# Hybrid retention/MoBA block: one Strassen unit of 512-column products for MoBA's values and the first retention gate, in place of two units of 256-column products

## The chip, the cores and the metric

The kernel runs on one core of one Trainium2 chip. The metric is the device time of one execution in microseconds (us), lower is better; it is given as the median of several executions. The engines are PE (TensorE: matmuls, and its weight loads as PEld), DVE (VectorE), ACT (ScalarE), POOL (GpSimd) and SP (SyncE, which here only issues transfers).

## The reference

One decoder layer in float32 on 512 tokens of width 1024:

```python
h = rmsnorm(x, norm1_w)
rq, rk, rv, rg, mq, mk, mv, ga, gb = split(h @ w_in)   # 512,512,1024,1024,512,512,512,1024,1024 columns
a = (silu(rg) * retention(rotary(rq), rotary(rk), rv)) @ w_ret_out     # 4 heads, 128 / 256 wide
b = moba_attention(rmsnorm(mq), rmsnorm(mk), mv) @ w_moba_out          # 8 heads of 64
x = x + (sigmoid(ga) * a + sigmoid(gb) * b) @ w_o
x = x + (silu(h2 @ w_ffn_gate) * (h2 @ w_ffn_up)) @ w_ffn_down         # h2 = rmsnorm(x, norm2_w)
```

With 512 tokens the MoBA selection takes every earlier block, so attention is plain causal attention. The change concerns the 512 columns `mv` and the first 512 of the 1024 columns `rg` (the gate of retention heads 0 and 1).

## The kernel before, in words

**Arithmetic.** Each float32 operand is split into a high and a low fp32r part, and each product is three matmuls (high x high, high x low, low x high: `mm3`). Most projections are done by Strassen's method (the class `Wino` keeps the sums of the activations): a unit makes four quarters of a result from seven quarter products instead of eight. The activations' pieces are kept for the whole first half. A weight piece is a tile of 128 x 1024 float32 (512 KB): it is loaded (`load_w`), where Strassen needs a sum of quarters a second transfer from POOL adds to it, or DVE adds two pieces (`make_sum`); then ACT writes the high part `wh` (line 418) and DVE the low part `wl`. Up to 3, sometimes 4, split pieces stand ahead of PE.

**Units.** `weight_plan` (line 87) lists the units in order. Kind "X" with 256-column halves gives 512 output columns: four quarters of 256 tokens x 256 columns. A product is one weight piece: 2 token tiles of 128 times 4 row tiles times 3 matmuls of 256 columns. Kind "X" with 512-column halves exists already for `w_o` and `w_ffn_down`: each quarter is 256 tokens x 512 columns, a product has two weight pieces and 2 x 2 x 2 x 3 matmuls of 512 columns, and each of its results takes two PSUM banks. `wino_prod` (line 780) issues a product and `wino_unit` (line 811) a unit. The order of the products is `NORMAL = "B11 T1 *1 T2 B21 B22 T3 / T4"`: the last one, T4, is put off and issued in the following unit, behind that unit's second product.

**Order of the work.** PE gets first the MoBA queries and keys (`tok_double`, 512-column matmuls), then the unit of `mv` (256-column, lines 1007 to 1020), then the units in the order of `ORDER` (line 44): rg0, rk0, rv0, gb0, rk1, rv1, rg1, gb1, b0, b1, ga0, a0, ga1, a1; then `w_o` and the feed-forward part. Here rk is a pair of rotary query and key units, ga and gb are the merge gates, a and b the two output projections.

**The background queue.** Everything else (norms, transposes, attention, retention) lies in one first-in, first-out list `bg`. `run_bg(1)` (line 708) takes one step of it after every 12 matmuls of 256 columns, or every 6 of 512 in a 512-column unit. This text calls such a place a slot. A 256-column unit has 14 slots, two to a product. The key's preparation takes 15 steps from the end of the key products on: 3 empty, `qk_scales`, four `k_norm`, 3 empty, four `k_transpose` (line 961). Attention's 38 steps (`att_step`) are appended by `mv_out` once the last quarter of `mv` is done, which is in unit rg0 behind T4. The steps of retention follow when `rv` is done (19 steps a pair of heads), and those of the gate (`gates`, line 1142) when `rg` and `rv` both are.

**Evacuation.** The class `Quarters` takes a 256-column unit's results out of PSUM: P1 is copied from bank X to bank Z (line 890), two negated intermediates go to SBUF (893, 896), DVE subtracts two, and the `out` function takes each finished quarter. `mv_out` scales by the row norm (line 1013), and `rg_unit` copies two of its quarters (line 1130).

**Space.** SBUF holds 47 tiles of 128 x 1024 float32, for weights and activations alike: a load waits until its slot is free. PSUM has 8 banks. One, `zbank`, is held from the start for bank Z. A side step (`side_ps`) takes a bank for itself. After the query unit `more_raws(EXTRA)` allows one more weight tile, 5 in all.

Of the kernel before, what the change touches and what calls it, by code (L numbers as in the profile page):

```python
# [38 lines left out]
PAHEAD = (6, 8)  # L39
STARTERS = 2  # L40
EXTRA = 1
OEXTRA = 5
FEXTRA = -2
ORDER = (("rg", 0), ("rk", 0), ("rv", 0), ("gb", 0), ("rk", 1), ("rv", 1), ("rg", 1), ("gb", 1), ("b", 0), ("b", 1), ("ga", 0), ("a", 0), ("ga", 1), ("a", 1))
RLAG = (1, 2, 3)
SLAG = (1, 1, 1)
ROT = 1
# [39 lines left out]
def weight_plan():  # L87

    units = []

    def feat(blocks):
        assert len(blocks) % 16 == 0  # L100
        for i in range(0, len(blocks), 16):
            units.append(("F", blocks[i:i + 16]))

    def group(name, col, kts):
        return [(name, k * P, col) for k in range(kts)]

    def wino(name1, col1, name2, col2, order=NORMAL):
        quarters = ((name1, col1, 0), (name2, col2, 0), (name2, col2, 4), (name1, col1, 4))
        units.append(("W", [(n, (k0 + k) * P, c + i * P) for n, c, k0 in quarters for i in (0, 1) for k in range(4)],
                      order))  # L110

    halves = (range(4), range(4, 8))

    def cols(col):
        units.append(("X", ("w_in", halves, col, 256), NORMAL))

    units += [("M", (C_MQ, 0)), ("M", (C_MQ, 4)), ("M", (C_MK, 0)), ("M", (C_MK, 4))]
    cols(C_MV)
    for name, i in ORDER:
        if name == "rg":  # L120
            cols(C_RG + 512 * i)
        elif name == "rv":
            cols(C_RV + 512 * i)
        elif name == "rk":
            wino("w_in", C_RQ + 256 * i, "w_in", C_RK + 256 * i)
        elif name == "a":
            feat(sum([group("w_ret_out", (4 * i + ct) * P, KT) for ct in range(4)], []))
        elif name == "b":
            feat(sum([group("w_moba_out", (4 * i + ct) * P, 4) for ct in range(4)], []))
        else:  # L130
            c = {"ga": C_GA, "gb": C_GB}[name] + 512 * i
            wino("w_in", c + 256, "w_in", c)
    units.append(("X", ("w_o", halves, 0, 512), ALONE))
    for c in range(len(CHUNKS)):
        fs = chunk_tiles(c)
        for f in fs[::2]:
            order = ENDING if f == fs[-2] else NORMAL
            if f < 4:
                order = (PLAIN, DOWN)[f // 2]
            wino("w_ffn_gate", f * P, "w_ffn_up", f * P, order)  # L140
        units.append(("X", ("w_ffn_down", (fs[::2], fs[1::2]), 0, 512), ALONE if c == len(CHUNKS) - 1 else DOWN))
    return units


# [25 lines left out]
def hybrid_block(ctx: ExitStack, tc: tile.TileContext, wall, xin, xtok, n2, cin, out):  # L170
# [15 lines left out]
    def big(name, dt=F32):  # L186
        return bp.tile([P, 1024], dt, name=name, tag="b")
# [14 lines left out]
    def main_ps():  # L202
        return pp.tile([P, 512], F32, name=nm("pm"), tag="bank")
# [7 lines left out]
    class Paced:  # L211


        def __init__(self, engine, cost):
            self.engine, self.cost = engine, cost
# [47 lines left out]
    def later(n, f):  # L263
        later_q.append([n, f])
# [454 lines left out]

    zbank = main_ps()  # L720

    def tok_double(mov, evac):

        pss = [main_ps() for _ in range(NT - 1)] + [main_ps() if cur[0] else zbank]
        lows = []
        for k in range(KT):
            for t in range(NT):
                m = ("A11", "A21", "A12", "A22")[k // 4 * 2 + t // 2]
                mm3(pss[t], tuple(x[:, t % 2 * P:t % 2 * P + P] for x in hW(m, k % 4)), mov(k), k == 0, k == KT - 1)
            advance(1)  # L730
            for l in lows:
                l()
            lows = [sums.pop(0)() for _ in range(SUMS) if sums and k < KT - 1 and cur[0]]
            run_bg(1)
        for t in range(NT):
            evac(t, pss[t])
        cur[0] += 2
# [73 lines left out]
    def wino_unit(w, ev, hooks={}):  # L811

        u = cur[0]
        cur[0] += 1
        order = plan[u][2].split()
        wide = plan[u][0] == "X" and plan[u][1][3] == 512
        banks = {}

        def bank(b):
            if b not in banks:  # L820
                z = zbank if b == "Z" else main_ps()
                banks[b] = [z, main_ps()] if wide else z
            return banks[b]

        def third(*x):
            ev.c22(*x)
            if "T4w" in order:
                ev.u3(*x)

        def first(*x):  # L830
            ev.p1(*([*x, bank("Z")] if seed else x))

        whole = "T4w" in order or "T4z" in order
        seed = not wide and order[1] != "B21"
        table = {"B11": ("X", "A11", True, False, first), "T1": ("Y", "S1", True, False, ev.p5),
                 "T2": ("X", "S2", False, False, ev.u2), "B21": ("Z", "A12", not seed, True, ev.c11),
                 "B22": ("Y", "S4", False, True, ev.c12), "T3": ("X", "S3", False, whole, third),
                 "T4": ("X", "A22", False, True, ev.c21),
                 "T4w": ("W", "A22", True, True, getattr(ev, "c21w", None)),
                 "T4z": ("Z", "A22", False, True, ev.c21)}  # L840

        def run(q):
            b, m, start, stop, out = table[q]
            wino_prod(w, u, bank(b), m, q.rstrip("wz"), start, stop, out,
                      bank("Z") if q == "T3" and "T4z" in order else None,
                      q == "T4z")

        rest = False
        for q in order:
            if q == "/":  # L850
                rest = True
            elif q[0] == "*":
                for _ in range(int(q[1:])):
                    wino_finish()
            elif rest:
                wpend.append(lambda q=q: run(q))
            else:
                run(q)
                if q in hooks:
                    hooks[q]()  # L860
# [22 lines left out]
    class Quarters:  # L883
# [27 lines left out]
        def c21(self, x):  # L911
            self.out(1, 0, x)


    mqT, mkT = {}, {}
    r1 = {}
# [59 lines left out]
        V.tensor_tensor(st["wqk"], vec[:, V_Q:V_Q + 1], vec[:, V_K:V_K + 1], ALU.mult)  # L976

    tok_double(lambda k: mw[k], qk_evac(0, qraw))
    more_raws(EXTRA)
    bg.append(norm1_rows)  # L980
    for g in range(4):
        bg.append(lambda g=g: q_transpose(g))
# [21 lines left out]
    for g in range(4):  # L1004
        bg.append(lambda g=g: k_transpose(g))

    mv = {}

    def mv_out(pair, u, x):
        for i in (0, 1):  # L1010
            t = 2 * pair + i
            mv[t, u] = (mv_ev.a, mv_ev.b)[u][:, t * 256:(t + 1) * 256]
            A.activation(mv[t, u], x[:, i * 256:(i + 1) * 256], AF.Copy, scale=st["r1"][:, t:t + 1])
        if (pair, u) == (1, 0):
            for n in range(len(items) + ATT[1]):
                bg.append(lambda n=n: att_step(n))

    wstate["cap"] = AHEAD
    mv_ev = Quarters(mv_out)
    wino_unit(hW, mv_ev)  # L1020


    srg_ev = {}
# [77 lines left out]
    def att_values(g):  # L1101

        ps = side_ps()
        for j in range(NT):
            for r in (0, 1):
                x, o = pt_tile(g, r, j)
                h = 2 * g + r
                T.matmul(ps[r * MDH:(r + 1) * MDH, j * P:], lhsT=mv[j, h // 4][:, h % 4 * MDH:(h % 4 + 1) * MDH],
                         rhs=x[:, o:o + S - j * P], start=j == 0, stop=j == NT - 1, skip_group_check=True)
        del pT[g]  # L1110
        moT[g] = split(f"moT{g}", ps, None, SLAG[0])
# [9 lines left out]
    moT = {}  # L1121


    srg = {}

    def rg_unit(n):
        def out(pair, i, x):
            if i == 0:
                y = ev.free if pair else ev.a[:, :512]
                A.copy(y, x)  # L1130
                x = y
            srg[2 * n + i, pair] = x
            if (pair, i) == (1, 0):
                gates(n)
                ret_done("rg")

        ev = Quarters(out)
        wino_unit(hW, ev)
# [164 lines left out]
    def ret_gate(h, pair):  # L1303
        x = srg[h, pair]
        for i in (0, 1):
            t = 2 * pair + i
            c = slice(i * 256, (i + 1) * 256)
            A.activation(x[:, c], x[:, c], AF.Silu, scale=st["r1"][:, t:t + 1])

    def ret_norm(h, pair):  # L1310
        o = ro[h, pair]
        for i in (0, 1):
            c = slice(i * 256, (i + 1) * 256)
            x = h * NT + 2 * pair + i
            A.activation(o[:, c], o[:, c], AF.Identity, scale=st["gn"][:, x:x + 1], bias=st["gb"][:, x:x + 1])
        later(1, lambda: V.tensor_tensor(o, o, srg[h, pair], ALU.mult))

    retT = {}

# [99 lines left out]
    def branch(cts, n, mov, evac):  # L1419
# [8 lines left out]
        "a": lambda n: branch(range(4 * n, 4 * n + 4), KT, retT, a_evac),  # L1428
        "b": lambda n: branch(range(4 * n, 4 * n + 4), 4, moT, b_evac),
    }  # L1430
    for name, n in ORDER:
        make[name](n)
    assert not bg
# [353 lines left out]
```

## Time and profile before

| | us |
|---|---|
| median of 3 runs | 779.98 (779.82 to 781.38) |
| the profiled execution, its own time | 780.48 |
| its span, first to last instruction | 778.4 |
| PE busy | 772.3 (99%) |
| DVE busy | 630.3 (81%) |
| ACT busy | 457.1 (59%) |
| POOL busy | 68.8 (9%) |

The profile is of one execution. Times count from the start of the span, which is some 2 us shorter than the execution. The granted TensorE clock is 0.999 on average. Line 222 is a helper through which all matmuls and most DVE instructions go, so they are told apart by their tiles: `pm` is a PSUM bank of the main products, `ps` one of a side step, `wh` and `wl` the parts of a weight piece, `raw` a weight piece as loaded.

### The profile page before, as it was taken

The numbers are of one execution on the slowest core, as the hardware profiler recorded it, in microseconds if no ns is written. First come the engines' busy times: TensorE is split into PE (matmuls) and PEld (weight loads), VectorE is DVE, ScalarE is ACT, GpSimd is POOL, SyncE is SP. The second block draws the span as 40 slices with busy tenths as digits, with TensorE's granted clock in tenths as the row PEclk, the third lists the DMA queues.
The fourth block names the chain that finished last, engine by engine and source line by source line (L and its number), as shares of the span: only waits on it lengthen the run. The fifth ranks groups of instructions, "written<-read, shape, count | busy, mean of one in ns | idle before, by whom it ended". The sixth has DMA issues, their size and how long they took to land.

```text
span 778.4 us, 13652 instructions
## 1 busy us (share of the span) xinstructions
PE 772.3 (99%) x5394; PEld 711.3 (91%) x5394; DVE 630.3 (81%) x959; ACT 457.1 (59%) x750; POOL 68.8 (9%) x83
## 2 busy tenths in 40 slices
PE   9999999999999999999999999999999999999997
PEld 6889988899999998989988899989999899988996
DVE  7988778897788687758589898899787987789787
ACT  8655677774695485635355675654554455654542
POOL 0000100010101000000001000111001110110000
PEclk9999999999999999999999999999999999999999
DMA  9854653556677484654899604789556894779502
GB/s 325 284 129 115 164 131 87 136 140 159 186 165 188 122 223 115 168 136 126 249 331 257 173 27 119 181 204 312 148 137 161 248 279 109 164 208 288 127 1 108
DMA packets 40671, 134.86 MB, mean 173 GB/s; under 512 B 4512, under 2 KB 5024, under 8 KB 40608
## 3 DMA queue, kind: packets, MB, share of 16 engines
q1 hardware_dynamic: 28512, 93.75, 34.4%
q0 software_dynamic: 11376, 39.06, 28.8%
q10 hardware_dynamic: 720, 1.18, 0.4%
q8 instruction: 42, 0.69, 0.3%
q14 instruction: 21, 0.17, 0.1%
HBM read 131.88 MB, written 2.10 MB: 172 GB/s over the span
## 4 chain that ended last, share of the span: by engine, by line
PE 88%; DVE 5%; issue 3%; DMA 2%; ACT 2%; POOL 0%; DVEq 0%; ACTq 0%; POOLq 0%
PE pm L222 79%; PE ps L222 8%; DMA raw<-wall 2%; DVE wl L222 1%; DVE h L222 1%; DVE ws L222 1%; ACT wh L418 0%; ACT f L1530 0%; DVE xr L222 0%; DVE xn L222 0%; DVE mx L222 0%; ACT h L1518 0%; POOL raw L345 0%; DVE qb L222 0%; DVE gsl L222 0%
## 5 line engine op out<-in xcount | busy, mean ns | idle before, releaser
L222 DVE TENSOR_TENSOR wl<-raw,wh 128x1024 fp32r<-128x1024 f32 x209 | 252.3, 1221 | 40.9 <-ACT wh L418 34.2
L418 ACT CAST wh<-raw 128x1024 fp32r<-128x1024 f32 (+1 forms) x230 | 225.3, 1007 | 52.2 <-DVE raw L222 26.5
L222 PE MATMUL pm<-h,wh 128*128 128x256 f32 x1248 | 225.5, 283 | 0.7 <-DVE h L222 0.5
L222 PEld LDWEIGHTS pm<-h,wh 128*128 128x128 f32 x1248 | 195.0, 192 | 1.7 <-DVE h L222 0.8
L222 PE MATMUL pm<-h,wl 128*128 128x256 f32 x624 | 176.6, 283 | 0.0
L222 PEld LDWEIGHTS pm<-h,wl 128*128 128x128 f32 x624 | 119.7, 192 | 0.0
L345 POOL DMA_DIRECT2D raw<-wall x60 | 55.2, 921 | 439.3 <-DMA raw<-wall 259.9
L222 PE MATMUL pm<-hS,wh 128*128 128x256 f32 x384 | 71.0, 285 | 0.0
L222 PE MATMUL pm<-wh,hA 128*128 128x256 f32 (+1 forms) x304 | 68.6, 310 | 0.0
L222 PE MATMUL pm<-wh,hS 128*128 128x256 f32 x320 | 62.5, 286 | 0.0
L222 PEld LDWEIGHTS pm<-hS,wh 128*128 128x128 f32 x384 | 60.0, 192 | 0.6 <-issue 0.3
L222 PE MATMUL pm<-hS,wl 128*128 128x256 f32 x192 | 54.3, 283 | 0.0
L222 PE MATMUL pm<-hA,wh 128*128 128x256 f32 x288 | 53.7, 285 | 0.0
L222 PEld LDWEIGHTS pm<-wh,hA 128*128 128x128 f32 x304 | 50.9, 191 | 2.8 <-issue 0.2
L222 PEld LDWEIGHTS pm<-wh,hS 128*128 128x128 f32 x320 | 51.5, 191 | 0.0
L222 DVE TENSOR_TENSOR raw<-raw,raw 128x1024 f32<-128x1024 f32 (+1 forms) x41 | 48.2, 1181 | 0.4
L222 PE MATMUL pm<-wl,hA 128*128 128x256 f32 (+1 forms) x152 | 46.4, 305 | 0.0
L222 PEld LDWEIGHTS pm<-hA,wh 128*128 128x128 f32 x288 | 45.2, 192 | 0.4
L222 PE MATMUL pm<-wl,hS 128*128 128x256 f32 x160 | 45.2, 283 | 0.0
L222 PE MATMUL pm<-hA,wl 128*128 128x256 f32 x144 | 40.7, 283 | 0.0
L222 PE MATMUL pm<-wh,gsh 128*128 128x512 f32 x112 | 39.8, 390 | 0.0
L222 PE MATMUL pm<-ret,wh 128*128 128x512 f32 x128 | 39.5, 390 | 0.0
(250 smaller groups left out, 1392.3 us busy)
## 6 DMA issues: line engine op xcount, KB each, us to landing
raw<-wall SPq DMA_DIRECT2D x155, 512.0 KB, 4.9
raw<-wall POOLq DMA_DIRECT2D x70, 512.0 KB, 7.4
raw<-wall SPq DMA_DIRECT2D x19, 256.0 KB, 3.9
raw<-wall POOLq DMA_DIRECT2D x9, 256.0 KB, 7.5
xr<-xtok SPq DMA_DIRECT2D x4, 512.0 KB, 7.2
x<-xin SPq DMA_DIRECT2D x7, 256.0 KB, 4.9
out<-xr SPq DMA_DIRECT2D x7, 256.0 KB, 2.1
raw<-wall ACTq DMA_DIRECT2D x4, 256.0 KB, 6.1
```

What stands on the lines that cost most here:

```text
L222: return f(out, *args, **kw)
L345: nc.gpsimd.dma_start(t[:, s], wall[c, :, s], accum_op=ALU.add)
L418: A.copy(h, src)
```

## The change

The units `mv` and rg0 become one "X" unit with 512-column halves, whose two halves of columns are `mv` and rg's first 512. The plan's "X" entry now names both column starts. `ORDER` loses its first entry. After the query unit 4 more weight tiles are allowed (`WIDE`), and given back after the new unit. A second bank is kept for Z from the start (`zbanks`); the key unit uses it. A 512-column unit in the order `NORMAL` now also seeds Z with P1. A new class `WideQuarters` evacuates token tile by token tile. `mv` gets tiles of its own, and the gate stays in the class's two tiles, as strided views. Attention's steps are appended when the last quarter of the new unit is done, which is in rk0 behind T4. (Not shown: the host's packing of the weights, the strided views in `rg_unit`, `ret_gate` and `ret_norm`, and the two other "X" entries, whose columns are as before.)

```diff
+WIDE = 4
-ORDER = (("rg", 0), ("rk", 0), ("rv", 0), ("gb", 0), ...
+ORDER = (("rk", 0), ("rv", 0), ("gb", 0), ...
...
-    cols(C_MV)
+    units.append(("X", ("w_in", halves, (C_MV, C_RG), 512), NORMAL))
...
+    zbanks = [zbank, main_ps()]
...
-        pss = [main_ps() for _ in range(NT - 1)] + [main_ps() if cur[0] else zbank]
+        pss = [main_ps() for _ in range(NT - 1)] + [zbanks[cur[0] // 2]]
...
-                banks[b] = [z, main_ps()] if wide else z
+                banks[b] = [z, zbanks.pop() if b == "Z" and len(zbanks) > 1 else main_ps()] if wide else z
...
-        seed = not wide and order[1] != "B21"
+        seed = order[1] != "B21"
...
+    class WideQuarters:
+        def __init__(self, out):
+            self.out = out
+            self.tiles = big(nm("qa")), big(nm("qb"))
+            self.a, self.b = ((t[:, :512], t[:, 512:]) for t in self.tiles)
+        def p1(self, x, i, z):
+            A.copy(z[i], x[i])
+        def p5(self, y, i):
+            A.activation(self.a[i], y[i], AF.Copy, scale=-1.0)
+        def u2(self, x, i):
+            A.activation(self.b[i], x[i], AF.Copy, scale=-1.0)
+        def c11(self, z, i):
+            self.out(0, 0, i, z[i])
+        def c12(self, y, i):
+            V.tensor_tensor(self.b[i], self.b[i], y[i], ALU.subtract)
+            later(1, lambda: self.out(0, 1, i, self.b[i]))
+        def c22(self, x, i):
+            V.tensor_tensor(self.a[i], self.a[i], x[i], ALU.subtract)
+            later(1, lambda: self.out(1, 1, i, self.a[i]))
+        def c21(self, x, i):
+            self.out(1, 0, i, x[i])
...
-    more_raws(EXTRA)
+    more_raws(EXTRA + WIDE)
...
+    def mv_rg_out(r, c, i, x):
+        t = 2 * r + i
+        if c == 0:
+            if i == 0:
+                mv[t], mv[t + 1] = halves(nm("mv"))
+            A.activation(mv[t], x, AF.Copy, scale=st["r1"][:, t:t + 1])
+            return
+        if i == 1:
+            for h in (0, 1):
+                srg[h, r] = two(mv_ev.tiles[1 - r])[:, :, h * 256:(h + 1) * 256]
+        if t == 3:
+            gates(0)
+            ret_done("rg")
             for n in range(len(items) + ATT[1]):
                 bg.append(lambda n=n: att_step(n))
...
+    wstate["cap"] = AHEAD
+    mv_ev = WideQuarters(mv_rg_out)
+    wino_unit(hW, mv_ev)
+    more_raws(-WIDE)
     for name, n in ORDER:
```

## Rows read from the trace of the kernel before

**Rows 1.** The page's busy us: share of the span, instructions

```profile
PE 772.3 (99%) x5394; PEld 711.3 (91%) x5394; DVE 630.3 (81%) x959; ACT 457.1 (59%) x750; POOL 68.8 (9%) x83
```

**Rows 2.** Stretches: busy us (instructions) by engine, clock, DMA share, GB/s

```profile
20.00:40.00 20.00, 20.00 (x98) 16.65 (x97) 19.17 (x38) 13.40 (x21) 1.87 (x2) 1.00 0.84 265
40.00:60.00 20.00, 20.00 (x122) 17.71 (x121) 17.15 (x29) 10.88 (x18) 1.76 (x2) 1.00 0.52 132
60.00:80.00 20.00, 20.00 (x171) 20.00 (x170) 16.18 (x29) 13.35 (x22) 1.51 (x3) 1.00 0.48 128
...
160.00:180.00 20.00, 20.00 (x161) 18.49 (x160) 16.74 (x24) 14.41 (x29) 2.35 (x3) 1.00 0.70 159
180.00:200.00 20.00, 20.00 (x165) 19.87 (x165) 15.95 (x31) 11.27 (x21) 1.40 (x2) 1.00 0.48 132
```

**Rows 3.** PE's waits: who waited for whom, us in total, times, longest

```profile
PE ps L542 <- DVE warm L222: 1.2, 1, 1.2
PE pm L222 <- DVE h L222: 0.5, 1, 0.5
PE pm L222 <- DVE ml L222: 0.2, 1, 0.2
```

**Rows 4.** The chain that ended last: start us, us, what

```profile
54.16 17.27 PE pm L222 x144
...
83.24 1.21 PE ps L222 x16
```

**Rows 5.** The chain from 48 to 60 us alone (end of the key products)

```profile
47.83 5.44 PE pm L222 x24
```

**Rows 6.** Groups by form on DVE: count, busy us, mean ns, idle before

```profile
L222 DVE TENSOR_TENSOR wl<-raw,wh 128x1024 fp32r<-128x1024 f32 x209 | 252.3, 1221 | 40.9 <-ACT wh L418 34.2 <-issue 4.5 <-ACT sc L1260 1.9
```

**Rows 7.** The same by form on ACT

```profile
L418 ACT CAST wh<-raw 128x1024 fp32r<-128x1024 f32 x209 | 214.3, 1047 | 47.4 <-DVE raw L222 26.5 <-DMA raw<-wall 16.5 <-PE pm L222 2.7
...
L893 ACT ACTIVATE qa<-pm 128x512 f32<-128x512 f32 x11 | 6.6, 596 | 0.1
...
L1130 ACT COPY qa<-pm 128x512 f32<-128x512 f32 x4 | 2.3, 583 | 0.0
...
L1013 ACT ACTIVATE qb<-qb,r_y 128x256 f32<-128x256 f32 x4 | 1.8, 500 | 1.8 <-DVE qb L222 1.8
...
L1013 ACT ACTIVATE qa<-pm,r_y 128x256 f32<-128x256 f32 x4 | 1.7, 472 | 2.5 <-PE pm L222 2.5
```

**Rows 8.** ACT in order of time: attention's table load, gb0's first tanh, gb1's load

```profile
85.20 1.28 ACT L1062 ACT_TABLE_LOAD   x1 [2.52 <-DVE nb L222]
...
183.63 0.63 ACT L1359 ACTIVATE qa<-qa 128x512 f32<-128x512 f32 x1
...
289.45 1.28 ACT L1359 ACT_TABLE_LOAD   x1
```

**Rows 9.** ACT's table loads at line 1359, whole span

```profile
L1359 ACT ACT_TABLE_LOAD x1 | 1.3, 1283 | 0.0
```

**Rows 10.** PE in order of time: first and last of the four key transposes

```profile
71.27 0.60 PE L222 MATMUL ps<-cst,qk 128*128 128x128 f32 x4
...
76.89 0.60 PE L222 MATMUL ps<-cst,qk 128*128 128x128 f32 x4
```

**Rows 11.** DVE in order of time: the low parts that free their banks

```profile
73.21 0.75 DVE L222 SCALAR_TENSOR_TENSOR mk<-ps,wqk,mk 128x512 fp32r<-128x512 f32 x1
...
78.97 0.75 DVE L222 SCALAR_TENSOR_TENSOR mk<-ps,wqk,mk 128x512 fp32r<-128x512 f32 x1
```

**Rows 12.** Waits of SP's queue, whole span

```profile
SPq L343 <- PE pm L222: 359.7, 96, 24.7
...
SPq L343 <- PE ps L222: 84.3, 15, 14.3
...
SPq L343 <- DVE rl L222: 12.2, 2, 8.7
```

**Rows 13.** The page's DMA issues: count, KB each, us to landing

```profile
raw<-wall SPq DMA_DIRECT2D x155, 512.0 KB, 4.9
raw<-wall POOLq DMA_DIRECT2D x70, 512.0 KB, 7.4
```

More of the change, by code (lines that the diff above doesn't have):

```diff
@@ L41 @@
 EXTRA = 1
+WIDE = 4
 OEXTRA = 5
 FEXTRA = -2
-ORDER = (("rg", 0), ("rk", 0), ("rv", 0), ("gb", 0), ("rk", 1), ("rv", 1), ("rg", 1), ("gb", 1), ("b", 0), ("b", 1), ("ga", 0), ("a", 0), ("ga", 1), ("a", 1))
+ORDER = (("rk", 0), ("rv", 0), ("gb", 0), ("rk", 1), ("rv", 1), ("rg", 1), ("gb", 1), ("b", 0), ("b", 1), ("ga", 0), ("a", 0), ("ga", 1), ("a", 1))
 RLAG = (1, 2, 3)
@@ L114, in cols @@
     def cols(col):
-        units.append(("X", ("w_in", halves, col, 256), NORMAL))
+        units.append(("X", ("w_in", halves, (col, col + 256), 256), NORMAL))
     units += [("M", (C_MQ, 0)), ("M", (C_MQ, 4)), ("M", (C_MK, 0)), ("M", (C_MK, 4))]
-    cols(C_MV)
+    units.append(("X", ("w_in", halves, (C_MV, C_RG), 512), NORMAL))
     for name, i in ORDER:
@@ L132, in weight_plan @@
             wino("w_in", c + 256, "w_in", c)
-    units.append(("X", ("w_o", halves, 0, 512), ALONE))
+    units.append(("X", ("w_o", halves, (0, 512), 512), ALONE))
     for c in range(len(CHUNKS)):
@@ L140, in weight_plan @@
             wino("w_ffn_gate", f * P, "w_ffn_up", f * P, order)
-        units.append(("X", ("w_ffn_down", (fs[::2], fs[1::2]), 0, 512), ALONE if c == len(CHUNKS) - 1 else DOWN))
+        units.append(("X", ("w_ffn_down", (fs[::2], fs[1::2]), (0, 512), 512), ALONE if c == len(CHUNKS) - 1 else DOWN))
     return units
@@ L1005, in hybrid_block @@
         bg.append(lambda g=g: k_transpose(g))
[L1007 to L1014, printed above, removed]
+    mv, srg = {}, {}
+    def mv_rg_out(r, c, i, x):
[11 more added lines that the diff above has]
+            ret_done("rg")
             for n in range(len(items) + ATT[1]):
                 bg.append(lambda n=n: att_step(n))
-    wstate["cap"] = AHEAD
-    mv_ev = Quarters(mv_out)
-    wino_unit(hW, mv_ev)
     srg_ev = {}
@@ L1107, in att_values @@
                 h = 2 * g + r
-                T.matmul(ps[r * MDH:(r + 1) * MDH, j * P:], lhsT=mv[j, h // 4][:, h % 4 * MDH:(h % 4 + 1) * MDH],
+                T.matmul(ps[r * MDH:(r + 1) * MDH, j * P:], lhsT=mv[j][:, h * MDH:(h + 1) * MDH],
                          rhs=x[:, o:o + S - j * P], start=j == 0, stop=j == NT - 1, skip_group_check=True)
@@ L1121, in hybrid_block @@
     moT = {}
-    srg = {}
     def rg_unit(n):
@@ L1131, in out @@
                 x = y
-            srg[2 * n + i, pair] = x
+            srg[2 * n + i, pair] = two(x)
             if (pair, i) == (1, 0):
@@ L1306, in ret_gate @@
             t = 2 * pair + i
-            c = slice(i * 256, (i + 1) * 256)
-            A.activation(x[:, c], x[:, c], AF.Silu, scale=st["r1"][:, t:t + 1])
+            A.activation(x[:, i], x[:, i], AF.Silu, scale=st["r1"][:, t:t + 1])
     def ret_norm(h, pair):
@@ L1315, in ret_norm @@
             A.activation(o[:, c], o[:, c], AF.Identity, scale=st["gn"][:, x:x + 1], bias=st["gb"][:, x:x + 1])
-        later(1, lambda: V.tensor_tensor(o, o, srg[h, pair], ALU.mult))
+        later(1, lambda: V.tensor_tensor(two(o), two(o), srg[h, pair], ALU.mult))
     retT = {}
@@ L1760 @@
         elif kind == "X":
-            name, (r0, r1), col, half = what[0]
-            for r, c in ((r0, col), (r0, col + half), (r1, col + half), (r1, col)):
+            name, (r0, r1), (c0, c1), half = what[0]
+            for r, c in ((r0, c0), (r0, c1), (r1, c1), (r1, c0)):
                 q = np.concatenate([w[name][k * P:(k + 1) * P, c:c + half] for k in r], axis=1)
```

## The prediction

> **What bounds the kernel now.** First the page's busy times: PE is busy 772.3 of 778.4 us [rows 1], with DVE second at 630.3. Busy matmuls overlap in this profile, so that alone proves little. Next the stretches: from 40 to 80 and from 160 to 200 us PE is busy 20.00 of each 20, while DVE leaves 2.8 to 4.1 us and ACT 5.6 to 9.1 [rows 2]. Then PE's own waits: over the whole span it waited for another engine's work 1.9 us in all [rows 3]. So there is no stall around these units that the change could remove. It can save only what PE itself spends, and it can add stalls. The granted clock is 1.00 in these stretches [rows 2], the 2.4 GHz level, so none is to be won there either.
>
> **What a matmul costs.** A mean duration does not tell, since matmuls overlap; the distance of their starts does. The chain shows the six products that the `mv` unit issues itself, 144 matmuls of 256 columns, in 17.27 us [rows 4]: 119.9 ns each. Just before, 24 matmuls of 512 columns of the key unit take 5.44 us [rows 5]: 226.7 ns. Those have the shape that the new unit issues, 128 token columns standing and 512 weight columns moving. At 2.4 GHz 256 columns are 106.7 ns and 512 are 213.3. So either form pays about 13.3 ns a matmul beyond its columns, and half the matmuls pay half of that.
>
> **PE's sum.** Removed: two units x 7 products x 24 = 336 matmuls x 119.9 ns = 40.30 us. Added: 7 products x 2 weight pieces x 12 = 168 x 226.7 ns = 38.08 us. The difference is -2.22 us. The same columns stream past, and the number of weight loads halves. Transposes, attention and retention keep their matmuls, and each step still cuts into the main stream once, so I cost those at zero.
>
> The Trainium skill has a rule against this (TensorE: Matmul & The Clock Gate, Back-to-back issue gap): warm, two matmuls start N/2.4 + 2.5 ns apart. By that two of 256 would cost 218.3 ns and one of 512 215.8, and the change would save an estimated 0.4 us. The rows differ from it, 119.9 where it has 109.2, so the sum stands on the rows.
>
> **Weight work.** Either plan has 14 weight pieces: 14 `wh` of 1047 ns on ACT and 14 `wl` of 1221 ns on DVE [rows 6, 7]. Either has two DVE sums for T2, ten plain loads and six adding ones. Nothing is added, but the pace rises: a piece lasts 12 x 226.7 ns = 2.72 us instead of 24 x 119.9 = 2.88. That is 6% more per us, and DVE's 16.18 of 20 would become some 17. I cost it at zero, hidden behind PE.
>
> **Evacuation.** ACT loses eight scalings of 472 to 500 ns and two copies of 583 (3.9 + 1.2 = 5.1 us), and gains four of 128x512, for which the nearest row is 596 ns (2.4 us) [rows 7]. DVE keeps its four subtractions. ACT is not what PE waits for: zero.
>
> **The four extra loads.** `WIDE` puts 4 x 512 KB = 2.1 MB behind the query unit. From 20 to 40 us the transfers run at 265 GB/s, from 40 to 60 at 132 [rows 2]; filling that gap takes 2.1 MB / 133 GB/s = 16 us, done near 56. The plan's first two pieces lie ahead of them in SP's queue, and the ones behind are used only from about 65 us on (54.2 + four pieces of 2.72). Zero, while slots are free; otherwise see the third rival.
>
> **Attention starts later.** Before, its steps enter `bg` after 12 slots of `mv`, 4 of rg0 and 2 of T4: slot 18, counted from the end of the key unit. After, it is 24 slots of the new unit, 4 of rk0 and 4 of T4: slot 32. With 38 steps it ends near slot 70 instead of 56, in rk1 instead of gb0. The first retention steps (19, appended at slot 60) then run from 70 to 89 instead of 60 to 79. The second batch is appended at 102 in either kernel, and the last 20 before the first output projection run as before. So one step still runs per slot: work is swapped between stages with the same DVE room (16.74 and 15.95 of 20 [rows 2]), and the delay is absorbed before slot 102. Attention's exponentials now meet gb0's tanh. That costs no table load: the tanh at 183.63 runs on the table loaded at 85.20, and line 1359 loads only once, at 289.45 [rows 8, 9]. Zero. A gain from the move is excluded too, since PE has no wait there.
>
> **Sum.** -2.2 us against the profiled execution's 780.48 gives 778.3. That execution lies 0.5 above the median of 779.98, so I forecast 777.8. The comparison can tell about 0.2%, 1.6 us, from no change.
>
> **Rival 1: PSUM takes it back.** Before, the `mv` unit holds three banks and five serve the side steps. The new unit holds six of eight until its results are out. The four key transposes come in slots 11 to 14, one per slot, now with two banks. One holds its bank from PE's start to the end of DVE's low part: 71.27 to 73.96 for the first, 76.89 to 79.72 for the last, 2.7 and 2.8 us [rows 10, 11]. The third transpose needs the first one's bank two slots later, 2 x (1.36 + 0.44) = 3.6 us; 0.44 is what four transposes add. That leaves 0.8. For it: one more `wh` and one `wl` in front (1.05 + 1.22 = 2.3 us [rows 6, 7]) would overrun it by 1.5 us. Against it: ACT and DVE are not full there. It gives 779.3, inside the bound of no change.
>
> **Rival 2: the columns are all that counts.** The 13.3 ns may not belong to each matmul. If they follow something that stays, the sums for T2 and the evacuations say, or PE's side steps, then 168 matmuls fewer save nothing: 780.0. Against it: both paces are read from undisturbed streams a few us apart [rows 4, 5]. The change would then not do what it says. By the Trainium skill's formula, named above, this rival would come out at an estimated 0.4 us saved.
>
> **Rival 3, slower: SBUF runs out.** All 47 slots are in use: SP's loads already wait 359.7 us in total for slots that PE frees, up to 14.3 for a side step's and up to 8.7 for one of attention's [rows 12]. Five weight tiles of 2.88 us give a load 14.4 us of cover; an added pair needs 4.9 + 7.4 = 12.3 us [rows 13], so 2.1 are spare. Attention's tiles now live 14 slots longer, beside two units of rotary and value tiles and a gate's, and SP's queue is in order: one stuck load holds all behind it. Once such a wait grows by more than 2.1 us, the next piece's `wh` and `wl` come late and PE stops. An added wait of 8.7 us costs 6.6, so -2.2 + 6.6 = +4.4: 784.4. Against it: no row of PE's waits names a piece so far [rows 3].
>
> **How the numbers follow.** The forecast has 0.62: both paces are measured and nothing else ends on PE. Rival 1 has 0.19, rival 2 0.04 (the traces speak against it), rival 3 0.15. The forecast's own range is 777.0 to 778.4, half a us of placing on either side and the spread between runs. The range given reaches over rivals 1 and 2 and the mild end of rival 3, 777.0 to 781.2; left out are most of rival 3 and a little below. Faster by over 0.2% is the forecast, 0.62; within 0.2% are rivals 1 and 2, 0.23; slower is rival 3, 0.15.
>
> **What would show it.** Right: the chain shows the new unit's matmuls at 0.227 us, 12 of them in 2.72; PE's waits stay near 1.9 us; PE has 168 instructions fewer; attention's first scores come near 100 us instead of 83.24 [rows 4]; and at the start of b0 and afterwards everything lies 2.2 us earlier. Rival 1 would show as PE or its weight loads waiting for the `mk` low parts between 65 and 80 us; rival 2 as starts of the new matmuls 0.24 us apart; rival 3 as PE waiting for `wl` or `wh`, with SP's waits longer, between 90 and 220 us. The forecast is wrong if PE waits appear in the new unit or in gb0 and rk1, or if the gain up to b0 is lost in the `w_o` stage, where loads crowd.

## The result and the profile after

The changed kernel takes **785.43 us** (median of 4 runs, 783.52 to 786.5) where the kernel before, in the same comparison, takes 780.44 (4 runs). The ratio is 1.0061, 95% interval 1.0049 to 1.0072: slower by 0.6%. The prediction was 777.8 with a range up to 781.2, so it was wrong in size and in sign. The profiled execution has a span of 783.1 us against 778.4.

The page's busy times answer to [rows 1]. PE has its 168 instructions fewer, yet its busy time is 0.5 us longer, with a stretch at half clock in it that cost 1.4 us (below):

```profile
PE 772.8 (99%) x5226; PEld 704.0 (90%) x5226; DVE 629.9 (80%) x959; ACT 455.6 (58%) x744; POOL 68.9 (9%) x83
```

The chain that ended last, from the end of the key products on, answers to [rows 4] (start us, us, what):

```profile
54.42 16.35 PE pm L223 x72
...
91.86 1.17 PE ps L223 x15
```

72 matmuls of 512 columns in 16.35 us are 227.1 ns each; the prediction had 226.7. The second row is attention's first batch of scores. Now the waits of PE, which answer to [rows 3] (who waited for whom: us in total, times, longest):

```profile
PE pm L223 <- DVE wl L223: 2.8, 2, 2.3
PE ps L543 <- DVE warm L223: 1.2, 1, 1.2
PE pm L223 <- ACT pt L1136: 0.5, 1, 0.5
PE pm L223 <- DVE mh L223: 0.5, 1, 0.5
PE pm L223 <- DVE h L223: 0.4, 1, 0.4
PE ps L223 <- ACT p L1099: 0.4, 1, 0.4
PE ps L223 <- ACT pt L1136: 0.3, 1, 0.3
```

Four kinds of wait are new. One, for `mh`, lies at 6 us, ahead of everything that was changed, and comes and goes between the runs (0.6 us in run 1, the kernel before with another queue). The others are for a weight piece's low part `wl`, for attention's exponentials `p` (line 1099), and for copies `pt` of its transposed probabilities (line 1136). The stretches tell where. First the kernel before (us, then busy time of PE, PEld, DVE, ACT, POOL with instructions, clock, DMA share, GB/s):

```profile
120.00:140.00 20.00, 20.00 (x171) 17.34 (x170) 17.47 (x42) 13.72 (x38) 0.86 (x1) 1.00 0.33 81
...
220.00:240.00 20.00, 20.00 (x169) 20.00 (x168) 17.06 (x23) 16.64 (x27) 2.59 (x3) 1.00 0.71 187
```

The same two stretches of the changed kernel, and a short one inside the second:

```profile
120.00:140.00 20.00, 19.34 (x160) 16.53 (x156) 18.39 (x44) 15.75 (x40) 1.60 (x2) 1.00 0.25 63
...
220.00:240.00 20.00, 17.70 (x138) 17.50 (x137) 15.63 (x23) 18.89 (x30) 1.76 (x2) 0.93 0.60 159
237.00:240.50 3.50, 3.50 (x19) 3.50 (x18) 3.46 (x5) 2.97 (x4) 0.49 (x1) 0.51 0.40 140
```

Following PE's main matmuls through the units gives the balance. The table, worked out from the start of each product in both traces, tells by how many us the changed kernel is later:

| place | later by |
|---|---|
| end of the key products | +0.26 |
| rv1's first product (attention and the first retention steps lie before it) | +1.25 |
| rv1's product B22 | +1.25 |
| rv1's product T3 | +5.05 |
| b0 | +5.30 |
| `w_o` and after, to the end | +4.96 |

The new unit's gain of some 2 us is thus lost before rv1, with 1 us more; and in one product of rv1 3.8 us go at once.

**What happens in rv1.** The SiLUs of the gate of heads 0 and 1 (line 1342) now run inside it, from 225.2 to 232.8 us, up to its product B22. ACT, DVE and PE of the changed kernel in order of time (start us, us, instruction, in brackets the idle time before it and who ended it):

```profile
223.86 1.28 ACT L1342 ACT_TABLE_LOAD   x1
...
230.92 1.03 ACT L419 CAST wh<-raw 128x1024 fp32r<-128x1024 f32 x1
231.86 0.91 ACT L1342 ACTIVATE qa<-qa,r_y 128x256 f32<-128x256 f32 x2
232.78 0.58 ACT L1216 COPY rot<-pm 64x512 f32<-64x512 f32 x1
233.37 0.58 ACT L1217 COPY rot<-pm 64x512 f32<-64x512 f32 x1
```

```profile
233.98 0.69 DVE L223 TENSOR_TENSOR rot<-pm,cs 128x512 f32<-128x512 f32 x1 [2.93 <-ACT rot L1217]
234.59 1.22 DVE L223 TENSOR_TENSOR wl<-raw,wh 128x1024 fp32r<-128x1024 f32 x1
```

```profile
235.86 0.39 PE L223 MATMUL pm<-wl,hS 128*128 128x256 f32 x1 [2.29 <-DVE wl L223]
```

The piece's high part is ready at 231.95, but DVE takes its work in order, and ahead of this `wl` stands a rotary step that waits for ACT's two copies, which stand behind a SiLU. So `wl` ends at 235.80, 2.5 us after PE asked for it at 233.28. The same place before:

```profile
223.75 0.90 ACT L1308 ACTIVATE qb<-qb,r_y 128x256 f32<-128x256 f32 x2
```

```profile
230.18 0.69 DVE L222 TENSOR_TENSOR rot<-pm,cs 128x512 f32<-128x512 f32 x1 [1.23 <-ACT rot L1182]
230.79 1.22 DVE L222 TENSOR_TENSOR wl<-raw,wh 128x1024 fp32r<-128x1024 f32 x1
```

The last SiLU had ended at 224.65, and `wl` ended at 232.004, while the piece's product began at 232.035. The lead, from the end of a piece's `wl` to the start of its product, was **0.03 us**: no wait, so none of the views read ahead of the prediction shows it, and nothing to spare. PE's weight loads show the same. Before, the load of this `wl` came 0.14 us after the one in front of it, where 0.12 is usual around it, and 0.05 us behind the end of `wl`; in the changed kernel it stood waiting and came 0.05 us behind it too. First before, then after:

```profile
231.92 0.19 PEld L222 LDWEIGHTS pm<-wh,hS 128*128 128x128 f32 x1
232.06 0.19 PEld L222 LDWEIGHTS pm<-wl,hS 128*128 128x128 f32 x1
```

```profile
235.86 0.19 PEld L223 LDWEIGHTS pm<-wl,hS 128*128 128x128 f32 x1 [2.50 <-DVE wl L223]
```

The leads of the pieces of rv1 from T1 to B22 (with rk1's T4 between) were 5.4, 5.2, 3.3, 1.5 and 0.03 us before; now they are 6.4, 5.1, 2.3, 1.4 and -2.5. So the pieces ahead are nearly as early as before, and it is this one that falls behind.

Right after its stall PE runs at half clock: the stretch from 237.0 to 240.5 has 0.51, the 1.2 GHz level, where [rows 2] have 1.00. There 15 matmuls take 3.21 us (237.19 to 240.40) instead of 15 x 119.9 ns = 1.80. So 3.8 = 2.4 of wait and 1.4 of clock.

**A misreading.** The text ahead of the result says that attention is appended in rk0 behind T4, in slot 32, near 100 us. By the diff it is appended with the last quarter, c22, which stands behind T3; T4 is put off. It enters the queue in slot 25, and the first scores come in slot 26, at 91.8 us, while the unit still holds its two X banks for T4.

### The profile page after: what moved, and what is told of

It reads as the page before. It is cut to its first block, busy times and chain, and to the rows that moved or that the text cites. A ratio compares the mean times of both kernels' runs of the same rounds, so it can differ in the third digit from the quotient of the medians.

```text
span 783.1 us, 13316 instructions
## 1 busy us (share of the span) xinstructions
PE 772.8 (99%) x5226; PEld 704.0 (90%) x5226; DVE 629.9 (80%) x959; ACT 455.6 (58%) x744; POOL 68.9 (9%) x83
## 4 chain that ended last, share of the span: by engine, by line
PE 76%; DVE 11%; ACT 6%; issue 4%; DMA 2%; POOL 0%; DVEq 0%; ACTq 0%; POOLq 0%
PE pm L223 71%; PE ps L223 5%; DVE wl L223 3%; DMA raw<-wall 2%; ACT wh L419 1%; DVE mx L223 1%; DVE rot L223 1%; DVE h L223 1%; ACT p L1099 1%; DVE ws L223 1%; DVE qb L223 0%; ACT f L1568 0%; ACT rot L1216 0%; DVE raw L223 0%; DVE p L223 0%
## 5 line engine op out<-in xcount | busy, mean ns | idle before, releaser
L223 PE MATMUL pm<-wh,hA 128*128 128x256 f32 (+1 forms) x256 | 66.8, 337 | 0.0
L223 PE MATMUL pm<-wh,hS 128*128 128x256 f32 (+1 forms) x256 | 58.7, 317 | 0.5 <-ACT pt L1136 0.5
L223 PEld LDWEIGHTS pm<-wh,hA 128*128 128x128 f32 x256 | 44.4, 190 | 4.1
L223 PEld LDWEIGHTS pm<-wh,hS 128*128 128x128 f32 x256 | 44.0, 196 | 3.4 <-ACT pt L1136 0.7
L223 PE MATMUL pm<-wl,hS 128*128 128x256 f32 (+1 forms) x128 | 40.4, 316 | 2.3 <-DVE wl L223 2.3
L223 PE MATMUL pm<-wl,hA 128*128 128x256 f32 (+1 forms) x128 | 42.2, 330 | 0.0
```

The source lines that it names most:

```text
L223: return f(out, *args, **kw)
```

## The experiments

The first question was which part costs: the side steps' new places, the space (rival 3), the banks, or the unit itself.

**1. Only the start of attention moved**, in the kernel before:

```diff
         if (pair, u) == (1, 0):
+            bg.extend([None] * 9)
             for n in range(len(items) + ATT[1]):
```

> The kernel before, with its two 256-column units, in which only the background queue is moved: nine empty steps ahead of attention, so that its first step falls behind the second half of rk0's first product, as in the changed kernel. Theory A (the loss comes from the place of the background steps, the wide unit itself saves its 2.2 us): slower than before by about what the changed kernel lost beside its saving, 4 to 7 us (784 to 787). Rival B (the loss comes from the wide unit's space, its PSUM banks and extra weight tiles): this kernel stays within 1 us of before.

Measured: 784.22 against 780.6, ratio 1.0049 [1.0037, 1.0061]. With no other edit the start of attention nine slots later costs 3.6 us. What stands behind attention in the queue moves with it: the first SiLU of heads 0 and 1 comes at 230.9 us instead of 218.5. PE's waits of this run, from the change on, that the kernel before doesn't have:

```profile
PE ps L222 <- ACT p L1063: 1.1, 2, 0.8
PE pm L222 <- ACT qb L896: 0.9, 1, 0.9
```

It waits for attention's exponentials, up to 120.1 and 160.9 us, and at 238.4, at rv1's T3, for an evacuation. 2.4 us are lost by rv1's T1 and 3.5 by b0. The part in rv1 falls among the SiLUs, which this edit moves too: the evacuation stands on ACT right behind the last of them.

```profile
236.99 0.90 ACT L1309 ACTIVATE qb<-qb,r_y 128x256 f32<-128x256 f32 x2
237.80 0.57 ACT L896 ACTIVATE qb<-pm 128x512 f32<-128x512 f32 x1
```

So the prediction's "zero" for the move is refuted by the move itself, without the new unit.

**2. Only the gate's SiLUs moved**, in the kernel before, by three slots: `RGATE = (5, 0)` for `(2, 0)`.

> The kernel before, with the SiLU steps of heads 0 and 1 three background steps later and nothing else moved. Theory A: the stall of the changed kernel in unit rv1 (PE waits 2.3 us for a low part, then runs at half clock for 3.4 us) comes from these eight SiLU activations meeting the pieces of rv1, whose lead in the kernel before is down to 0.03 us; 1.5 to 4 us slower than before. Rival B: no difference over 0.5 us, since nothing of the space changes.

Measured: 781.77, ratio 1.0016 [1.0007, 1.0025], 1.2 us. The trace puts it at 232.1 us, in rv1's B22, where PE now waits 1.1 us for `wl`: the piece with the lead of 0.03 us.

**3. The gate's SiLUs ahead of attention**, in the changed kernel (`gates` then does nothing for heads 0 and 1):

```diff
+                later(1 + h, lambda h=h: ret_gate(h, r))
         if t == 3:
-            gates(0)
             ret_done("rg")
```

> The changed kernel, with the SiLU of heads 0 and 1 issued as soon as the wide unit has the gate's quarters, ahead of attention, with one table load more. Theory A: the stall in rv1 is gone and PE runs rv1 at full clock, so about 3.8 us faster than the changed kernel (781.0 to 782.5), still slower than before by what attention's stretch lost. Rival B: no gain, 785 +- 1.

Measured: 787.48, ratio 1.0094 [1.0079, 1.0108]: a miss, 2 us slower than the changed kernel. The stall in rv1 goes (+0.3 us there instead of +3.8), but at attention's start the exponentials now stand behind table loads and SiLUs, and PE stops, in one piece, then runs at half clock:

```profile
PE ps L223 <- ACT p L1099: 4.0, 1, 4.0
```

```profile
99.80:106.60 6.80, 4.95 (x16) 3.76 (x17) 3.38 (x7) 6.74 (x11) 0.86 (x1) 0.50 0.50 80
```

**4. No extra weight tiles**, `WIDE = 0`.

> The changed kernel without its four extra weight tiles (WIDE 0, five tiles in all as before). Theory A: no gain in attention's stretch and in rv1; the wide unit has fewer loads ahead and may wait for them, 785 to 790. Rival B (the extra tiles take slots and make later loads late): faster than the changed kernel by 2 us or more, 783.5 or less.

Measured: 785.04, ratio 1.0064 [1.0047, 1.008], the changed kernel's time, with stalls in the same places. The four extra tiles play no part. That attention's tiles live longer, the other half of rival 3, this run doesn't test.

**5. The gate's SiLUs twelve slots later**, `RGATE = (14, 0)` in the changed kernel.

> The changed kernel, with the SiLU of heads 0 and 1 twelve background steps later, in unit rg1, where the pieces' lead is 2 to 8 us. Theory A (the SiLU steps meet the pieces of rv1): no wait for a low part in rv1 and full clock there, 3 to 4 us faster than the changed kernel, 781.0 to 782.5. Rival D (rv1 stalls because the retention steps ahead of it come late, whatever SiLU does): the stall stays, 784 to 786.

Measured: 781.26 (10 runs, 780.49 to 783.11) against 780.66, ratio 1.0012 [1.0003, 1.0022]. Compared each with its own kernel before, 4.4 us of the changed kernel's 5.0 are gone. The profile is of the slowest of the ten (783.11); even there the wait for `wl` is 1.3 us in two, and no stretch is at half clock. One of the two, 0.8 us, is still at rv1's B22, where theory A had expected none.

**6. T4 at once**, so that the X banks come free before attention:

```diff
 NORMAL = "B11 T1 *1 T2 B21 B22 T3 / T4"
+ATONCE = "B11 T1 *1 T2 B21 B22 T3 T4"
...
-    units.append(("X", ("w_in", halves, (C_MV, C_RG), 512), NORMAL))
+    units.append(("X", ("w_in", halves, (C_MV, C_RG), 512), ATONCE))
```

> The changed kernel, with the wide unit's T4 issued at once behind T3, not put off into rk0. Attention then starts over the end of the wide unit, with six side banks in place of three. Theory C (attention's stretch loses because the two X banks of the wide unit are still held when it starts): the waits of the first scores and of rv0's banks shrink, 1 to 2 us faster than the changed kernel. Theory A: attention still ends in gb0 and SiLU still falls into rv1, so within 1 us of the changed kernel, whatever the first 0.6 us wait does.

Measured: 784.52 (782.58 to 786.02), ratio 1.0051 [1.0032, 1.007]. The wait at 97.3 us, where scores stood without a bank, is gone; rv1 begins +0.18 us late instead of +1.25; the stall in rv1 remains (`wl` 2.1 us). So the banks do matter, at attention's first scores and not at the key transposes, for about 1 us.

**7 and 8. Attention left out** of both kernels (its steps stay as empty ones, so the order of everything else is kept), to see the unit alone. 7 is the kernel before, 8 the changed one.

```diff
     def att_step(n):
-        for f, lag in ((att_transpose, ATT[0]), (att_scores, 0)):
-            if 0 <= n - lag < len(items) and items[n - lag]:
-                f(*items[n - lag])
         m = n - ATT[1]
         if 0 <= m < len(items) and items[m] and items[m][1:] == ((1,), NT - 1):
-            att_values(items[m][0])
+            moT[items[m][0]] = mqT[items[m][0]]
```

> The kernel before without attention's scores, softmax, transposes and values (the MoBA branch takes its queries in their place); the steps stay in the queue as empty ones. With e8 it measures the wide unit alone. Attention's matmuls take some 35 us of PE here, so about 745 us; no PE wait up to the merge gates.

> The changed kernel without attention, as in e7. All theories agree on the term of the sum: PE's chain up to the start of rk0 is 2.2 us shorter than in e7, less what the wide unit itself waits. If the unit's banks or loads cost something by themselves (rival B), it shows as PE waits ahead of rk0 and as less than 1.5 us saved. In total 1.5 to 2.5 us faster than e7, unless SiLU still stalls rv1, where theory A leaves 2 to 4 us to lose.

Measured: 748.41 and 747.76. From the end of the key products to rk0's T2, the first stage behind the unit in both orders, 8 takes 2.0 us less than 7. Up to rv1 it is 2.5, most of the rest being a stop of 7 itself, 0.3 us for a `wl` at 128.8 us. In rv1 1.3 us go again, in B22, with this wait of 8:

```profile
PE pm L223 <- DVE wl L223: 1.0, 1, 1.0
```

So the unit saves what the sum said, to a tenth (2.0 for 2.2), and the SiLUs' new place costs something even without attention.

**9 to 11. Another unit under attention.** If rk0's rotary work is what attention collides with, a unit without it should take its place: `ORDER` begins with gb0 (9), with gb0 and T4 at once (10), or with rg1, and with gb0 moved behind rv1 (11).

```diff
-ORDER = (("rk", 0), ("rv", 0), ("gb", 0), ("rk", 1), ("rv", 1), ("rg", 1), ("gb", 1), ...
+ORDER = (("gb", 0), ("rk", 0), ("rv", 0), ("rk", 1), ("rv", 1), ("rg", 1), ("gb", 1), ...
```

> The changed kernel with the merge-gate unit gb0 moved ahead of rk0, so that attention starts over a unit without rotary work, as it did over rg0 in the kernel before, and so that the first SiLU steps fall between rv1 and rg1. Theory A (the wide unit saves 2.2 us, and what is lost is lost by where the background steps meet the units): attention's stretch loses 1 us at most and rv1 nothing beyond 1 us, so 778 to 780.5, faster than before or the same. Rival E (the loss goes with attention starting while the wide unit's T4 is still due, wherever rk0 stands): 2 us lost again in attention's stretch, 781 to 784.

> As e9, with the wide unit's T4 at once behind T3. Theory A: 0.5 to 1 us faster than e9, by the first wait of the scores, which the pair of changed kernel and e6 showed as 0.9 us: 777.5 to 780. Rival E: the larger part of attention's loss goes with it, 2 us faster than e9.

> The changed kernel with unit rg1 ahead of rk0 and both merge gates behind rv1, so that attention starts over a plain gate unit as in the kernel before and the first SiLU steps fall into gb0. Theory A: attention's stretch loses 1 us at most; the second SiLU steps now meet gb0's tanh, one or two more table loads of 1.28 us, so 778 to 781. Rival E: 781 to 784.

Measured: 781.56 (1.0011 [1.0002, 1.002]), 780.72 (1.0002 [0.9993, 1.0011]) and 781.89 (1.0018 [1.0009, 1.0027]). All are 3.5 us or more better than the changed kernel, and all miss what was expected: none gets under the kernel before. Run 10 waits 1.7 us for `wl` in two places, 170.1 and 222.2 us; run 11 waits for exponentials. The waits move with the order.

**12. T4 at once and the late gate together** (the edits of 5 and 6).

> The changed kernel with T4 at once (e6) and the first SiLU steps twelve steps later (e5), the order of the units unchanged. Theory A: the two gains add, 0.9 and 4.1 us off the changed kernel's 785.4, so 780 to 781: the wide unit's saving is then still given back by attention over rk0. Rival: with both waits gone the saving shows, 778.5 or less.

Measured: 780.7, ratio 1.0001 [0.9992, 1.001]: the gains add. PE's waits that are left, beside the ones of the kernel before:

```profile
PE pm L224 <- DVE wl L224: 0.8, 2, 0.5
...
PE pm L224 <- ACT pt L1137: 0.5, 1, 0.5
PE ps L224 <- ACT pt L1137: 0.3, 1, 0.3
```

In its PE stream the excess gaps are 0.68 at 128.2 us, 0.45 and 0.19 near 139, 0.69 at 171.5 and 0.40 at 232.2: 2.4 us, about the unit's whole saving.

**13 to 16. More pieces ahead.** If the small lead is the cause, one more split piece ahead of PE (`AHEAD = (4, 4)` for `(3, 4)`) should help: on 10 (13), on the kernel before (14), on 12 (15); 16 is 13 with `HLAG = 0` for 1.

> e10 (gb0 first, T4 at once), with four split pieces ahead of PE at all times. Theory F (what is left is the pieces' lead): the two waits of 1.0 us for low parts near 170 and 222 us go, 778 to 779.5, faster than before. Rival G (ACT and DVE are simply full there): 780 to 781.5, as e10.

> The kernel before, with four split pieces ahead of PE at all times: a control. It has no wait for a low part to lose, so both theories expect no gain; within 0.7 us of before, or slower if the fourth pair of tiles makes loads late.

> e12 (the changed kernel's order, T4 at once, SiLU late), with four split pieces ahead at all times. Theory F: the waits of 0.7 and 0.4 us for low parts at 171 and 232 us go, those for a bank (0.7 at 128) and for the transposes (0.6 at 139) stay, 779 to 780. Rival G: 780.2 to 781.2, as e12.

> e13, with T2's high part issued at once behind its sum instead of one step later. Theory F: T2's pieces come 1.4 us earlier, the same as e13 or up to 1 us faster. Rival G: ACT stands waiting for DVE's sum with other work behind it, slower than e13 by 0.5 to 2 us.

Measured: 782.27 (1.0024 [1.0015, 1.0034]), 781.49 (1.0012 [1.0003, 1.0021]), 781.2 (1.0012 [1.0003, 1.0021]) and 787.4 (1.0093 [1.008, 1.0107]). In 13 and 15 no wait for `wl` is left, yet they are 1.5 and 0.5 us slower than 10 and 12. Run 13 waits in their place for ACT:

```profile
PE pm L224 <- ACT pm L894: 1.1, 2, 0.6
PE ps L224 <- ACT p L1100: 0.8, 1, 0.8
PE ps L224 <- ACT pt L1132: 0.8, 1, 0.8
```

Run 14, the control, loses its 1.1 us in rv0, under attention, and also to ACT (0.4 for `pt`, 0.3 for `p`), not to loads. Run 16 is worse than rival G had it: PE waits 3.3 us for one evacuation, then runs 3.4 us at half clock. Weight pieces made earlier are side work and evacuations made later. That fits ACT and DVE having too little room in these stretches, whichever of their work goes first; the next two runs test it. The theory that the lead alone is the cause falls.

**17 and 18. Less work under attention.** rk0's rotary work (ACT's copies and DVE's products and sums) is left out of the kernel before (17) and of run 12 (18); the quarters are only split, and at once.

```diff
+            if h0 == 0:
+                a = x
+                high()
+                later(1, lambda: V.tensor_tensor(part["L"], two(x), part["H"].bitcast(F32), ALU.subtract))
+                return
             d = lane_start(LANE)
```

> The kernel before with the rotary embedding of the first pair of retention heads left out (unit rk0's quarters are only split into high and low): 8 half-width ACT copies of 0.6 us and 12 DVE instructions of 0.69 us fewer in the stretch where attention runs. PE had no wait there, so within 0.7 us of before.

> e12 (changed kernel, T4 at once, SiLU late) with the same rotary work left out. Theory G (attention meets rk0's rotary work on ACT and DVE, and PE's waits there eat the saving): the waits near 128, 139 and 171 us go, 1.3 to 2.2 us faster than e17. Rival H (the waits belong to the order of the banks or to the wide unit): equal to e17 within 0.7 us, as e12 is to before.

Measured: 779.61 (0.9986 [0.9977, 0.9995]) and 778.22 (0.997 [0.996, 0.9981]). Run 17 gains more than the 0.7 us that were expected, and run 18 falls where theory G had it. Taking that work out gives the kernel before 1.1 us and run 12 2.5; the new unit, worth nothing with the work there (12 against before), is worth 1.4 us without it (in the profiled spans 2.6, 777.9 to 775.3). The stretch from 120 to 140 us, first of run 12, then of 18:

```profile
120.00:140.00 20.00, 19.10 (x160) 16.70 (x158) 18.41 (x42) 15.73 (x41) 1.73 (x2) 1.00 0.25 55
```

```profile
120.00:140.00 20.00, 20.00 (x171) 17.08 (x169) 15.87 (x38) 14.57 (x37) 1.84 (x2) 1.00 0.55 132
```

DVE at 18.41 of 20 goes with a PE that stops for 0.9; at 15.87 PE doesn't stop.

No version with the whole computation beats the kernel before: 10 and 12 equal it.

## Why the prediction was wrong, point by point

- **PE's sum** was right: 227.1 ns a matmul for 226.7, and 2.0 us saved for 2.2 where nothing else interferes (7 and 8). The rule of the Trainium skill that was weighed against it (TensorE: Matmul & The Clock Gate, Back-to-back issue gap) would have given an estimated 0.4 us; the traces differ from it (119.9 and 227.1 ns where it has 109.2 and 215.8). The Trainium skill itself calls that formula, in the same section, the isolated gap of a single matmul, which leaves out the weight loads of a real stream, so it was no rule against this sum. Rival 2 fell with the measured saving.
- **The extra loads** at zero were right (4). Rival 3, the slower one, had the right sign by a wrong mechanism: PE waits for `wl`, but the pieces ahead of it in rv1 are nearly as early as before. One load does land late: ACT stands 2.7 us for it up to 211.3 us (0.2 before), and 3.1 in run 12. It doesn't make the large stall, since the piece of that load, T1's, still leads by 6.4 us; whether the smaller waits that are left in rv1 in runs 5 and 12 go back to it is open.
- **Rival 1**, the banks, had the wrong place: PE doesn't wait at the key transposes. About 1 us went for banks at attention's first scores (6), because the steps start before T4, which the text had misread.
- **"Attention starts later": the step that failed.** It said that work is swapped between stages with the same room and that the delay is absorbed, cost zero. In the kernel before, nine slots cost 3.6 us (1), 2.4 of them ahead of rv1's T1. Between the key products and rv1 the changed kernel loses 3.0 us to it (+1.25 - 0.26, and the 2.0 saved), about 1 of them for the banks: attention and rk0's rotary steps already overlapped before (ACT's rotary copies run from 124 to 151 us inside attention's exponentials from 87 to 161), but the move shifts them against each other by some 17 us (116 to 144 inside 95 to 171). In the new arrangement ACT and DVE are late with one or the other, and without the rotary work most of the unit's saving comes through, 1.4 us between 17 and 18 where run 12 has none.
- **A step not seen.** The prediction followed attention and retention, and not what follows them in `bg`: the SiLUs of heads 0 and 1. The last of them ended 7.4 us ahead of rv1's B22 and now ends 0.5 ahead. It cost 3.8 us in one place (2.4 of wait, 1.4 of clock), and moving the SiLUs further back gave 4.4 back (5).
- **The reason behind both.** "PE waited 1.9 us in all, so there is no stall" was read as "there is room". Waits of zero say that nothing was late, not by how much it was early. DVE's 16 to 17 of each 20 us [rows 2] didn't say it either, since the wait is one of order: `wl` behind a rotary step behind ACT's copies behind a SiLU. In the kernel before, the lead of gb0's first piece was 0.20 us, that of rv1's B22 0.03, that of the next 1.17. The prediction named waits in gb0 and rk1 among what would make it wrong; the ones that came are in rk0 to gb0, and the largest in rv1.

**Open.** The rotary work was taken from ACT and DVE at once, so which of the two binds in 120 to 175 us was not separated; nor was it followed step by step why the new arrangement of the same work is worse than the old. No run moves attention without the steps behind it in the queue, so the 2.4 us of run 1 are not divided between attention and retention. Why the orders of 9 and 11 stay above the kernel before was followed only to the waits named.

## What to carry to other kernels

Half as many matmuls of twice the columns did save their 13 ns each here, but the time showed it only where PE is what the stage ends on. Before moving background steps, list for each prepared piece how long before PE's need it is finished: a wait table of zeros and a busy share of 80% can hide a lead of 0.03 us on an in-order queue. Follow every step behind the moved one in the same queue to its new place, and look at what the engine's next evacuation or weight piece stands behind there.

## What the runs showed of the hardware that was not expected

A stall of PE of 2 to 4 us may or may not be paid twice. In the changed kernel a wait of 2.3 us was followed by 3.4 us at the 1.2 GHz level, in run 16 one of 3.3 us also by 3.4 us, and in run 3 one of 4.0 us by 6.8 us (clock 0.50). But in run 4, in the same place of the program, a wait of 3.0 us was followed by full clock:

```profile
PE pm L223 <- DVE wl L223: 3.5, 2, 3.0
```

```profile
237.00:242.00 5.00, 5.00 (x43) 5.00 (x44) 4.97 (x7) 3.94 (x6) 0.86 (x1) 1.00 0.32 109
```

Run 6 also stays at full clock after 2.1 us. Only one execution of each kernel was profiled, but the mean granted clock is on record for every execution, and it settles that the clock falls in some executions of one kernel and not in others. The six executions of run 4 lie between 783.70 us with a clock of 1.000 and 788.75 us with 0.995, and of the four of run 8 three have 1.000 (747.24 to 748.07 us) and one 0.995 (751.74 us). All four of the changed kernel have 0.996 to 0.998, where the kernel before has 0.999 or 1.000.
